# Mask products first, then score and value products by alternating halves of the array, in a kernel for one step of a hybrid decoder

## The chip, the cores and the metric

The kernel runs on one core of a Trainium2 chip. The metric is the device time of one execution in microseconds (us). In the profile PE is TensorE's matmuls, PEld its weight loads, DVE VectorE, ACT ScalarE, POOL GpSimd, SP the engine that issues most DMAs.

## The reference

One layer of a decoder with two head groups works on 272 prompt positions (16 learned meta tokens and 256 of the prompt) and 8 sample sequences of one new token each. Cut to what matters here:

```python
z = h @ w_in                                  # u | q | k | v
y_ssm = s5_mixer(u, ...)                      # state-space heads
# sliding-window attention, 16 query heads of 64 on 4 key/value heads
s = einsum('bnqkgd,bnskd->bnkgqs', qb, k2) * HEAD_DIM ** -0.5
s = where(mask, s, -1e30)                     # causal, window 128
p = softmax over the keys and one learned sink per head
o = einsum('bnkgqs,bnskd->bnqkgd', p, v2)
x = x + concat(rmsnorm(y_ssm), rmsnorm(o)) @ w_out
x = x + conv_ffn(rmsnorm(x))                  # 2048 -> 2 x 5632 -> 2048
```

The meta positions, the prompt and the sample tokens go through the same layer; the attention of the sample tokens runs over a cache of 128 keys.

## The kernel before

Activations stand with features on the partitions and the 280 positions as columns. Every projection (`project`) takes its weights in chunks of 512 KB: one DMA to `w`, a rounding copy `wh` on ScalarE (L216) and the remainder `wl` on VectorE (L72 by way of `sub`), and then three products for each block, wh with the high part of the input, wh with the low part, wl with the high part (`mm3`, L233 to L235, tile `acc`). One chunk is 24 such matmuls in the attention stage. There are two buffers each of wh, wl and acc.

The attention of the prompt is done in eight groups (`att_group`), one for each of four key/value heads kv and of two blocks of 128 queries. Kind A, the first block, has 144 keys (16 meta keys with the values vM, which lie in the tile vx, and 128 with the values vA); kind B, the second, has 256 keys (vA and vB). A group has four query heads r and runs in four steps, with a `yield` between them:

1. Scores in the PSUM tile `sps`, two banks of 2 x 256 columns; head r goes to bank r % 2. For each head a bf16 product of the identity and the mask `maskb` writes the mask (L840), with all 128 rows of the array, and an fp32 product of `qT` and `kd` adds the scores (L841). Head dimension 64 fills half of the rows: heads 0 and 2 the lower half, heads 1 and 3 the upper.
2. Softmax: maximum on VectorE (L849), exponential on ScalarE (L856), sums, reciprocal (L860), scaling on ScalarE (L862). P has one buffer.
3. Eight transposes to `ppt` (L870) and two copies to `pt` on ScalarE (L873). sps and ppt share two PSUM buffers ("big").
4. Values in the one PSUM tile `ops` (L879): for each half `par` of the output partitions, that is of the array's columns, the two blocks of keys are accumulated. `att_out` then reads it with ScalarE and VectorE (L810, L811, L814).

All fp32 products run as two passes; a row of the trace that has x2 for one product in the code shows them.

TensorE's order is the order of the code (`manual_schedule`); the other engines' orders are set by the scheduler's priorities. The main loop (L1004) writes step 1 of a group, projection chunks of u (`us`, counted by the table UD), steps of the sample's and the meta tokens' attention (`side`, tiles ssp, p, osp and mps, mtp, mop), step 3 of the group before, step 2 of this one, again chunks of u, and step 4 of the group before. Between them VectorE builds tables for the state-space part (BB, CC) in pieces of low priority.

The stage lies between the projections of q and the state-space part. Behind it come the state-space part mixed with the output projection of the attention (oa), the gate, the rest of the output projection and the feed-forward part, which take 220 to 1200 us.

Of the kernel before, what the change touches and what calls it, by code (L numbers as in the profile page):

```python
# [65 lines left out]
def body(ctx, tc, I, O, dbg=None):  # L66
    nc = tc.nc
    dbg = dbg or {}
    V, A, G, PE = nc.vector, nc.scalar, nc.gpsimd, nc.tensor

    def tt(o, a, b, op, eng=V):
        return eng.tensor_tensor(o, a, b, op=op)  # L72

    def add(o, a, b, eng=V):
        return tt(o, a, b, OP.add, eng)
# [4 lines left out]
    def mul(o, a, b, eng=V):  # L80
        return tt(o, a, b, OP.mult, eng)
# [51 lines left out]
    identb = ap.tile([128, 128], BF, name="identb")  # L133
    G.tensor_copy(identb, ident)
    mf = stp.tile([128, 256], F32, name="mf")
    maskb = {}
# [167 lines left out]
    qT = buf[:, 0:8, :]  # L304
    bflat = buf.rearrange("p f n -> p (f n)")
    b8_ = bflat[:, 8 * NR:]
    kd = b8_[:, :4 * T].rearrange("p (f n) -> p f n", f=4)
# [497 lines left out]
    def att_out(f, src, c, n):  # L805

        m = src.shape[1]
        for a in range(m):
            g = vcol("attn_out_g", f + a)
            A.activation(ah[:, f + a, c:c + n], src[:, a], AF.Copy, scale=g)  # L810
            V.scalar_tensor_tensor(al[:, f + a, c:c + n], src[:, a], g, ah[:, f + a, c:c + n].bitcast(F32),  # L811
                                   op0=OP.mult, op1=OP.subtract)
        z = small.tile([128, T], F32, name="osqt", tag="tb")[:, :m * n].rearrange("p (a b) -> p a b", a=m)
        A.activation(z, src, AF.Square)  # L814
        o = osq[:, c:c + n]
        if f == 0:
            add(o, z[:, 0], z[:, 1], eng=G)
        for a in range(2 if f == 0 else 0, m):
            add(o, o, z[:, a], eng=G)
# [11 lines left out]
    def att_group(nm, kv):  # L831
        ci = 0 if nm == "A" else 1
        q0 = QC[ci][1]
        nk = 144 if nm == "A" else 256
        k0 = 0 if nm == "A" else 16
        sps = big.tile([128, 2, 2, 256], F32, name="sps", tag="big")
        for r in range(4):
            h = 4 * kv + r
            p = slice(64 * (h % 2), 64 * (h % 2) + 64)
            PE.matmul(sps[:, r % 2, r // 2, :nk], identb, maskb[nm][:, :nk], start=True, stop=False)  # L840
            PE.matmul(sps[:, r % 2, r // 2, :nk], qT[p, h // 2, q0:q0 + 128], kd[p, kv, k0:k0 + nk], start=False, stop=True)  # L841
        st = aw.tile([128, 8, 4], F32, name="st")
        mx, nm_, se, den, rec = (st[:, i, :] for i in range(5))
        yield
        hp = tc.high_priority()
        hp.__enter__()
        sk = sinks[:, 4 * kv:4 * kv + 4]
        sc = rq[:, 16 * ci + 4 * kv:16 * ci + 4 * kv + 4]
        V.tensor_reduce(mx.rearrange("p (a b) -> p a b", b=2), sps[:, :, :, :nk].rearrange("p b a k -> p a b k"),  # L849
                        axis=AX.X, op=OP.max)  # L850
        mul(nm_, mx, nrq[:, 16 * ci + 4 * kv:16 * ci + 4 * kv + 4])
        tt(nm_, nm_, nsk[:, 4 * kv:4 * kv + 4], OP.min)
        add(se, sk, nm_)
        P = aw.tile([128, 4, 256], F32, name="P", bufs=1)
        for r in range(4):
            A.activation(P[:, r, :nk], sps[:, r % 2, r // 2, :nk], AF.Exp, scale=sc[:, r:r + 1], bias=nm_[:, r:r + 1],  # L856
                         accum_out=den[:, r:r + 1])
        A.activation(se, se, AF.Exp)
        add(den, den, se)
        V.reciprocal(rec, den)  # L860
        for r in range(4):
            A.activation(P[:, r, :nk], P[:, r, :nk], AF.Copy, scale=rec[:, r:r + 1])  # L862
        hp.__exit__(None, None, None)
        yield
        blocks = ((0, 16, vM), (16, 128, vA)) if nm == "A" else ((0, 128, vA), (128, 128, vB))
        pts = []
        ppt = big.tile([128, 2, 4, 128], F32, name="ppt", tag="big")
        for bi, (c, n, vv) in enumerate(blocks):
            for r in range(4):
                PE.transpose(ppt[:n, bi, r, :], P[:, r, c:c + n], ident)  # L870
        for bi, (c, n, vv) in enumerate(blocks):
            pt = aw.tile([128, 4, 128], F32, name="pt")
            A.copy(pt[:n], ppt[:n, bi])  # L873
            pts.append(pt)
        yield
        ops = msc.tile([128, 2, 128], F32, name="ops", tag="msc")
        for par in range(2):
            for bi, (c, n, vv) in enumerate(blocks):
                PE.matmul(ops[64 * par:64 * par + 64], vv[:n, 64 * kv:64 * kv + 64], pts[bi][:n, par::2, :],  # L879
                          start=bi == 0, stop=bi == 1)  # L880
        att_out(2 * kv, ops, q0, 128)
        yield
# [65 lines left out]
    def att_meta():  # L948
# [41 lines left out]
        yield  # L990

    gs_ = [att_group(nm, kv) for nm in ("A", "B") for kv in range(4)]
    sg, mg = att_sample(), att_meta()
    def side(k):
# [437 lines left out]
```

## Time and profile before

| | |
|---|---|
| median of 3 runs | 1202.74 us (1202.39 to 1205.45) |
| profiled execution | 1202.62 us, span of its instructions 1200.4 us |
| PE busy | 1172.8 us, 98% of the span |
| PEld, DVE, ACT, POOL busy | 94%, 68%, 51%, 8% |
| granted TensorE clock, mean | 0.987 of 2.4 GHz |
| DMA | 201.90 MB, 168 GB/s |

In a timeline a row is one instruction or a run of like ones: its start, its length, what it writes and reads, how many there are, and in brackets how long the engine sat idle before it and which instruction ended that. Matmuls overlap each other, so what one costs is read from the start of a row to the start of the next and not from its length.

### The profile page before, as it was taken

The numbers are of one execution on the slowest core, as the hardware profiler recorded it, in microseconds if no ns is written. First come the engines' busy times: TensorE is split into PE (matmuls) and PEld (weight loads), VectorE is DVE, ScalarE is ACT, GpSimd is POOL, SyncE is SP. The second block draws the span as 40 slices with busy tenths as digits, with TensorE's granted clock in tenths as the row PEclk, the third lists the DMA queues.
The fourth block names the chain that finished last, engine by engine and source line by source line (L and its number), as shares of the span: only waits on it lengthen the run. The fifth ranks groups of instructions, "written<-read, shape, count | busy, mean of one in ns | idle before, by whom it ended". The sixth has DMA issues, their size and how long they took to land.

```text
span 1200.4 us, 23033 instructions
## 1 busy us (share of the span) xinstructions
PE 1172.8 (98%) x9184; PEld 1133.7 (94%) x9184; DVE 813.0 (68%) x1469; ACT 608.4 (51%) x1009; POOL 97.1 (8%) x243
## 2 busy tenths in 40 slices
PE   7999999899998999999999999999999999999998
PEld 6887878799997999999999999999999999999998
DVE  8798767488778967676767644446767676764443
ACT  5567557566564654454445433334445444543332
POOL 1020121322014200000000000000000000000000
PEclk9999889799999999999999999999999999999999
DMA  8445344434465655555555555555555555556664
GB/s 272 142 140 169 98 129 145 135 87 118 114 184 158 193 160 178 179 179 180 178 176 176 169 181 187 180 182 178 180 181 179 178 176 176 176 187 199 201 198 128
DMA packets 237114, 201.90 MB, mean 168 GB/s; under 512 B 16152, under 2 KB 233256, under 8 KB 236968
## 3 DMA queue, kind: packets, MB, share of 16 engines
q1 hardware_dynamic: 233856, 193.88, 52.9%
q10 hardware_dynamic: 2608, 3.58, 0.9%
q0 software_dynamic: 544, 2.97, 0.7%
q8 instruction: 72, 1.18, 0.5%
q14 instruction: 34, 0.28, 0.1%
HBM read 194.59 MB, written 8.25 MB: 169 GB/s over the span
## 4 chain that ended last, share of the span: by engine, by line
PE 91%; DVE 3%; ACT 3%; issue 1%; DMA 1%; SPq 0%; POOL 0%; ACTq 0%; DVEq 0%; POOLq 0%
PE acc L233 27%; PE acc L235 26%; PE acc L234 26%; PE yps L1136 2%; PE sps L841 2%; PE kvb L571 1%; DVE wl L72 1%; PE ops L879 1%; PE kps L1077 1%; ACT wh L216 1%; PE ppt L870 1%; PE vps L1095 1%; PE sps L840 1%; PE lps L1067 0%; DMA w<-w_in 0%
## 5 line engine op out<-in xcount | busy, mean ns | idle before, releaser
L72 DVE TENSOR_TENSOR wl<-w,wh 128x1024 fp32r<-128x1024 f32 (+1 forms) x348 | 419.8, 1206 | 306.4 <-ACT wh L216 302.2
L216 ACT CAST wh<-w 128x1024 fp32r<-128x1024 f32 (+1 forms) x348 | 358.2, 1029 | 493.4 <-PE acc L234 332.4
L233 PE MATMUL acc<-x2h,wh 128*128 128x266 f32 x1408 | 397.0, 287 | 0.7 <-DVE os L72 0.7
L234 PE MATMUL acc<-x2l,wh 128*128 128x266 f32 x1408 | 395.7, 286 | 0.0
L235 PE MATMUL acc<-x2h,wl 128*128 128x266 f32 x1408 | 375.0, 287 | 0.0
L234 PEld LDWEIGHTS acc<-x2l,wh 128*128 128x128 f32 x1408 | 267.1, 190 | 0.1
L233 PEld LDWEIGHTS acc<-x2h,wh 128*128 128x128 f32 x1408 | 265.9, 189 | 0.9 <-issue 0.9
L235 PEld LDWEIGHTS acc<-x2h,wl 128*128 128x128 f32 x1408 | 254.2, 189 | 0.1
L234 PE MATMUL acc<-hl,wh 128*128 128x264 f32 x704 | 196.1, 284 | 0.0
L233 PE MATMUL acc<-hh,wh 128*128 128x264 f32 x704 | 196.0, 284 | 0.0
L235 PE MATMUL acc<-hh,wl 128*128 128x264 f32 x704 | 184.2, 284 | 0.0
L234 PEld LDWEIGHTS acc<-hl,wh 128*128 128x128 f32 x704 | 132.3, 188 | 0.0
L233 PEld LDWEIGHTS acc<-hh,wh 128*128 128x128 f32 x704 | 132.3, 188 | 0.0
L235 PEld LDWEIGHTS acc<-hh,wl 128*128 128x128 f32 x704 | 126.1, 188 | 0.0
L233 PE MATMUL acc<-xh,wh 128*128 128x266 f32 (+1 forms) x256 | 78.8, 308 | 0.0
L235 PE MATMUL acc<-xh,wl 128*128 128x266 f32 (+1 forms) x256 | 75.9, 296 | 1.7 <-DVE wl L72 1.5
L234 PE MATMUL acc<-xl,wh 128*128 128x266 f32 (+1 forms) x256 | 75.8, 296 | 0.0
L1314 POOL COPY coll<-up 128x10 f32<-128x10 f32 x88 | 16.9, 192 | 634.1 <-DVE up L72 633.9
L233 PEld LDWEIGHTS acc<-xh,wh 128*128 128x128 f32 x256 | 50.3, 196 | 4.4 <-issue 3.4
L235 PEld LDWEIGHTS acc<-xh,wl 128*128 128x128 f32 x256 | 49.9, 195 | 2.4 <-DVE wl L72 2.3
L234 PEld LDWEIGHTS acc<-xl,wh 128*128 128x128 f32 x256 | 50.2, 196 | 0.1
L1317 ACT ACTIVATE ct<-up,cin 128x256 f32<-128x256 f32 x88 | 48.1, 594 | 0.0
(371 smaller groups left out, 1579.5 us busy)
## 6 DMA issues: line engine op xcount, KB each, us to landing
w<-w_up SPq DMA_DIRECT2D x176, 512.0 KB, 3.5
w<-w_down SPq DMA_DIRECT2D x64, 512.0 KB, 3.4
w<-w_in SPq DMA_DIRECT2D x40, 512.0 KB, 3.7
w<-w_out SPq DMA_DIRECT2D x32, 512.0 KB, 3.8
w<-w_down SPq DMA_DIRECT2D x32, 384.0 KB, 3.2
w<-w_glu SPq DMA_DIRECT2D x8, 512.0 KB, 3.7
buf<-x_t SPq DMA_DIRECT2D x4, 532.0 KB, 6.8
out_y<-buf ACTq DMA_DIRECT2D x8, 264.0 KB, 4.1
```

The costliest lines, as they stand in the source:

```text
L72: return eng.tensor_tensor(o, a, b, op=op)
L216: A.copy(wh[:, :nk, :], w[:, :nk, :])
L233: PE.matmul(ps, wh, xh, start=st, stop=False)
L234: PE.matmul(ps, wh, xl, start=False, stop=False)
L235: PE.matmul(ps, wl, xh, start=False, stop=sp)
L571: PE.matmul(kv_ps[f], kw[b][:, j, cc], xs[:, b + j, :], start=b + j == 0, stop=False)
L840: PE.matmul(sps[:, r % 2, r // 2, :nk], identb, maskb[nm][:, :nk], start=True, stop=False)
L841: PE.matmul(sps[:, r % 2, r // 2, :nk], qT[p, h // 2, q0:q0 + 128], kd[p, kv, k0:k0 + nk], start=False, stop=True)
L870: PE.transpose(ppt[:n, bi, r, :], P[:, r, c:c + n], ident)
L1136: PE.matmul(yps[:, r, :], lhs, rhs, start=part == 0, stop=part == 2)
L1314: G.tensor_copy(coll[:, n, :], up[:, NR - 10:NR])
L1317: A.activation(t, up[:, 2:258], AF.Identity, scale=cin[:, n, 2:3], bias=cin[:, n, 3:4])
```

## The change

All mask products of a group come first: one for each bank, with the mask read twice by a broadcast, so two products of 2 x nk columns instead of four of nk. The four score products follow, one behind the other, and only the last one on each bank closes its accumulation. In the values' products the two loops change places: block by block, the two halves of the columns one after the other.

```diff
         sps = big.tile([128, 2, 2, 256], F32, name="sps", tag="big")
+        for b in range(2):
+            PE.matmul(sps[:, b, :, :nk], identb, maskb[nm][:, None, :nk].to_broadcast([128, 2, nk]), start=True, stop=False)
         for r in range(4):
             h = 4 * kv + r
             p = slice(64 * (h % 2), 64 * (h % 2) + 64)
-            PE.matmul(sps[:, r % 2, r // 2, :nk], identb, maskb[nm][:, :nk], start=True, stop=False)
-            PE.matmul(sps[:, r % 2, r // 2, :nk], qT[p, h // 2, q0:q0 + 128], kd[p, kv, k0:k0 + nk], start=False, stop=True)
+            PE.matmul(sps[:, r % 2, r // 2, :nk], qT[p, h // 2, q0:q0 + 128], kd[p, kv, k0:k0 + nk], start=False, stop=r >= 2)
...
         ops = msc.tile([128, 2, 128], F32, name="ops", tag="msc")
-        for par in range(2):
-            for bi, (c, n, vv) in enumerate(blocks):
+        for bi, (c, n, vv) in enumerate(blocks):
+            for par in range(2):
                 PE.matmul(ops[64 * par:64 * par + 64], vv[:n, 64 * kv:64 * kv + 64], pts[bi][:n, par::2, :],
                           start=bi == 0, stop=bi == 1)
```

Lines behind the change are numbered one higher in the changed kernel (L841 becomes L842, L879 becomes L880).

On TensorE, the scores of the first group of kind A before, from the last small products ahead of them (qtp), for two of the four heads:

```order
L772 MATMUL qtp<-ones,qd 128x1
L840 LDWEIGHTS identb
L840 MATMUL sps<-maskA,identb 128x144
L841 MATMUL sps<-buf 128x144
L840 LDWEIGHTS identb
L840 MATMUL sps<-maskA,identb 128x144
L841 MATMUL sps<-buf 128x144
```

The same place now, with the whole group and the projection behind it (buf is the tile that holds qT and kd):

```order
L772 MATMUL qtp<-ones,qd 128x1
L838 LDWEIGHTS identb
L838 MATMUL sps<-maskA,identb 128x2x144
L838 LDWEIGHTS identb
L838 MATMUL sps<-maskA,identb 128x2x144
L842 MATMUL sps<-buf 128x144 x4
L233 MATMUL acc_1265<-xh,wh 128x280
```

Masks and scores no longer alternate, and the four score products stand in a row.

On TensorE, the values of the first group of kind A before, between a projection and the next group's mask:

```order
L235 MATMUL acc_1422<-xh,wl 128x280
L879 MATMUL ops<-pt,vx 64x256
L879 MATMUL ops<-pt,vA 64x256
L879 MATMUL ops<-pt,vx 64x256
L879 MATMUL ops<-pt,vA 64x256
L840 LDWEIGHTS identb
```

And now:

```order
L235 MATMUL acc_1418<-xh,wl 128x280
L880 MATMUL ops<-pt,vx 64x256 x2
L880 MATMUL ops<-pt,vA 64x256 x2
L838 LDWEIGHTS identb
L838 MATMUL sps<-maskA,identb 128x2x144
```

Products of the same block are now neighbours; in kind B the same holds for vA and vB.

On ScalarE, whose order the scheduler sets, before, from the table load ahead of the first exponentials to the second group's scaling:

```order
L856 ACT_TABLE_LOAD
L856 ACTIVATE P,st<-sps,st,rq 128x144 x4
L858 ACTIVATE st<-st 128x4
L216 CAST wh<-w 128x1024
L862 ACTIVATE P<-P,st 128x144 x4
L858 ACTIVATE st<-st 128x4
L856 ACTIVATE P,st<-sps,st,rq 128x144 x4
L873 COPY pt<-ppt 16x512
L873 COPY pt<-ppt 128x512
L216 CAST wh<-w 128x1024
L967 ACTIVATE mS<-mS 2x256
L969 ACTIVATE mst<-mst 2x16
```

And now:

```order
L857 ACT_TABLE_LOAD
L857 ACTIVATE P,st<-sps,st,rq 128x144 x4
L859 ACTIVATE st<-st 128x4
L216 CAST wh<-w 128x1024
L863 ACTIVATE P<-P,st 128x144 x2
L859 ACTIVATE st<-st 128x4
L863 ACTIVATE P<-P,st 128x144 x2
L857 ACTIVATE P,st<-sps,st,rq 128x144 x4
L874 COPY pt<-ppt 16x512
L874 COPY pt<-ppt 128x512
L968 ACTIVATE mS<-mS 2x256
L970 ACTIVATE mst<-mst 2x16
```

The head of the row is the same; the weight cast that stood behind the copies of pt has moved behind the next group's scaling.

## Rows read from the trace of the kernel before

**Rows 1.** The page, the chain that ended last: shares of the span by engine.
```profile
PE 91%; DVE 3%; ACT 3%; issue 1%; DMA 1%; SPq 0%; POOL 0%; ACTq 0%; DVEq 0%; POOLq 0%
```

**Rows 2.** Waits of PE, 104.7 to 217 us: total, times, longest.
```profile
PE ppt L870 <- ACT P L862: 0.9, 1, 0.9
```

**Rows 3.** Busy time by stretch: PE, PEld, DVE, ACT, POOL; granted clock; DMA.
```profile
104.70:141.05 36.35, 35.39 (x267) 28.04 (x267) 30.62 (x93) 27.48 (x67) 4.09 (x7) 1.00 0.46 137
141.05:147.90 6.85, 6.85 (x27) 5.77 (x27) 3.28 (x9) 0.39 (x1) 1.04 (x2) 0.51 0.25 73
161.50:164.90 3.40, 3.40 (x17) 3.40 (x16) 2.45 (x7) 2.89 (x10) 1.93 (x4) 0.50 0.48 152
175.20:182.00 6.80, 6.80 (x24) 4.97 (x24) 3.65 (x9) 1.07 (x2) 2.16 (x4) 0.50 0.62 183
178.35:194.98 16.63, 16.63 (x101) 14.09 (x102) 14.17 (x32) 8.58 (x23) 2.81 (x6) 0.89 0.37 107
104.70:217.00 112.30, 110.66 (x717) 86.67 (x716) 81.43 (x213) 69.93 (x183) 20.03 (x40) 0.90 0.47 145
```

**Rows 4.** Timeline of PE: scores of the first group of kind A.
```profile
104.78 0.24 PE L840 MATMUL sps<-maskA,identb 128*128 128x144 bf16 x1
104.95 0.51 PE L841 MATMUL sps<-buf 64*128 64x144 f32 x2
105.39 0.24 PE L840 MATMUL sps<-maskA,identb 128*128 128x144 bf16 x1
...
107.21 0.40 PE L233 MATMUL acc<-xh,wh 128*128 128x280 f32 x1
```

**Rows 5.** Timeline of PE: scores of a group of kind B.
```profile
188.29 0.28 PE L235 MATMUL acc<-xh,wl 128*128 128x280 f32 x1
188.42 0.28 PE L840 MATMUL sps<-maskB,identb 128*128 128x256 bf16 x1
188.63 0.70 PE L841 MATMUL sps<-buf 64*128 64x256 f32 x2
189.26 0.28 PE L840 MATMUL sps<-maskB,identb 128*128 128x256 bf16 x1
...
191.78 0.40 PE L233 MATMUL acc<-xh,wh 128*128 128x280 f32 x1
```

**Rows 6.** PE, 116.11 to 116.14; statistics of L952 (ns, min/median/max); the first transposes.
```profile
116.12 0.18 PE L952 MATMUL mps<-buf 64*2 64x16 f32 x2
...
L952 PE MATMUL mps<-buf x32: 172/173/175, 116.1 to 116.5; 64*2 64x16 f32 x32
...
117.56 1.63 PE L870 MATMUL ppt<-ident,P 128*16 128x128 f32 x8 [0.88 <-ACT P L862]
```

**Rows 7.** Timeline of PE: values of the first group of kind A.
```profile
122.21 0.64 PE L879 MATMUL ops<-pt,vx 16*64 16x256 f32 x2
122.78 0.65 PE L879 MATMUL ops<-pt,vA 128*64 128x256 f32 x2
...
124.50 0.24 PE L840 MATMUL sps<-maskA,identb 128*128 128x144 bf16 x1
```

**Rows 8.** Timeline of PE: values of the first group of kind B.
```profile
184.21 0.66 PE L879 MATMUL ops<-pt,vA 128*64 128x256 f32 x4
184.69 0.61 PE L879 MATMUL ops<-pt,vB 128*64 128x256 f32 x4
185.23 0.40 PE L233 MATMUL acc<-xh,wh 128*128 128x280 f32 x1
```

**Rows 9.** Timeline of ACT before the first transposes.
```profile
111.88 1.28 ACT L856 ACT_TABLE_LOAD   x1
...
116.14 1.04 ACT L216 CAST wh<-w 128x1024 fp32r<-128x1024 f32 x1 [0.95 <-ACT st L858]
117.09 1.33 ACT L862 ACTIVATE P<-P,st 128x144 f32<-128x144 f32 x4
```

**Rows 10.** Timeline of DVE: scaling of the sample's probabilities.
```profile
194.23 0.28 DVE L925 TENSOR_SCALAR Ps<-Ps,sst 128x128 f32<-128x128 f32 x1
```

## The prediction

> **What bounds the kernel now.** I read the page first, for the share of each engine and the chain that ended last: 91% of it is TensorE [rows 1]. Nearly all of that is the projections, which the change leaves alone; the touched work lies in the attention stage, 104.7 to 217 us, so I then read that stretch by stages and by waits. There the longest wait of TensorE is 0.9 us [rows 2]; VectorE is busy 81.4 and ScalarE 69.9 of the 112.3 us [rows 3]. What TensorE saves there is therefore saved for the whole program, until another engine is late. After the stage the order of every engine is the same in both programs, and the feed-forward part that follows is TensorE's, so what is left at 217 us I carry to the end unchanged. Three stretches of the stage, 6.85, 3.40 and 6.80 us long, ran at half the clock (granted 0.50 to 0.51: 1.2 instead of 2.4 GHz) with TensorE busy throughout [rows 3]. Last I read the touched instructions one by one.
>
> **Scores.** In a group of kind A (144 keys) one head takes 0.17 us from the start of its mask product to that of its scores, and 0.44 from there to the next mask; four take 104.78 to 107.21, 2.43 us [rows 4]. In kind B (256 keys) the two are 0.21 and 0.63, and the group 3.36 [rows 5]. The difference of 112 columns gives the price of a column: 0.04/112 = 0.36 ns in the mask product, and 0.19/224 = 0.85 ns in one pass of the scores (each score product is two passes, the x2 of its row). What is left is fixed: 0.12 us for a mask product and 0.195 for a score product (0.44 - 288 x 0.85 ns). In the projections, where one full-array product follows another, a row starts 0.13 us after the last [rows 5], so the fixed part is hidden there; here it is paid at each change between the full array and a half of it, eight times in a group.
>
> After the change a group has one such change and back. Kind A: two mask products of 288 columns, 0.12 + 2 x 0.104 = 0.33 us (0.12 more if the second one's load isn't hidden). Then four score products, two on each half of the rows. Do the halves run side by side? The 32 meta products alternate halves in the same way: two that start at 116.12 together end 0.18 us later [rows 6], one alone takes 0.173 [rows 6], so they start at most 10 ns apart, less than the 16 x 0.85 = 14 ns in which one streams its columns. I take yes. Then the four cost 0.195 + 4 x 144 x 0.85 ns = 0.685, and the group 1.01 instead of 2.43: **1.42 saved**. In turn they would cost 1.175, with 0.93 saved. Kind B: 0.12 + 2 x 0.184 + 0.195 + 4 x 256 x 0.85 ns = 1.55 instead of 3.36: **1.81 saved**, 0.94 in turn. Four groups of each: 4 x (1.42 + 1.81) = **12.9 us**, lower end 7.5.
>
> **Values.** In kind A the four products start 0.57 us apart, 122.21 to 124.50, 2.29 in all [rows 7]: two passes of 256 columns at 0.85 ns are 0.435, the other 0.135 fixed, since vx fills 16 rows and vA 128 and each product follows one of the other kind. The change puts the two halves of vx together and then the two of vA. Two halves of one kind run side by side already: in kind B, whose two blocks both have 128 rows, the old order vA, vB, vA, vB shows as four passes of vA from 184.21 and four of vB from 184.69, done by 185.23, 1.02 us in all [rows 8], where eight passes in turn would be 1.74. So kind A becomes two pairs of 0.57, 1.14: 1.15 saved, four times, **4.5 us** after 0.02 for each pair's offset (ends 0, if halves of 16 rows don't pair, and 5.1, if it becomes as fast as B). In kind B I expect nothing.
>
> All this takes it that a pass may start ahead of earlier ones of the other half, as the four-and-four of [rows 8] shows: the program's order there is two passes of vA and two of vB on one half and then the same on the other. The Trainium skill (TensorE: Matmul & The Clock Gate, Part 3, What overlaps and what doesn't) says that matmuls start and end strictly in program order; the trace speaks against it here, and what it would make of the time is the fifth rival.
>
> **What is given back.** Sum so far 17.4 us of TensorE. Three items where another engine is then late:
> - The first transposes, ppt at 117.56, waited 0.88 us for the scaled probabilities [rows 6]. ScalarE's table load begins at 111.88; then come the exponentials and one weight cast, which stood 0.95 us until a projection freed its buffer; then the scaling, 117.09 to 118.4 [rows 9]. TensorE comes 2 x 1.42 = 2.84 us earlier, ScalarE only by that 0.95 (the scheduler still has table load, exponentials, cast and scaling in this order, and puts the next cast behind the second scaling). **1.9 lost.** The next values hang on that transpose by the exponentials and the copies of the probabilities, so they don't regain it.
> - The transpose of the sample's probabilities, p, needs VectorE's product Ps, started at 194.23 [rows 10], behind the products that build CC. From 178.35 to 194.98 VectorE works 14.2 of 16.6 us [rows 3]. TensorE would need 16.6 - 1.8 (scores) - 1.8 (half of the 3.65 us at half clock up to 182.0) = 13.0. At 14.5 for VectorE **1.5 lost** (0 if the clock stays, 2.6 if its idle time stays too).
> - The rest of the stage: TensorE goes from 112.3 to about 90 us, VectorE keeps its 81. I allow **1.5** (0 to 4) for scalings, copies and weight parts that come late.
>
> **The clock.** Each of the three falls came where no projection had run for some time: values, the 16 meta transposes and scores up to 141.05; scores, 16 sample products and transposes up to 161.5; values, sample products and scores up to 175.2. Projections brought it back. They cost half of 6.85 + 3.40 + 6.80, 8.5 us [rows 3]. The first of these stretches shrinks to about half (2.29 and 2.43 us of it become 1.14 and 1.01), so I take its 3.4 as won; of the others (5.1), whose sample products stay, half; and 1 is lost to a new fall at the longer wait before the first transposes: **+5.0** (ends 0 and 8.5).
>
> Sum: 12.9 + 4.5 - 1.9 - 1.5 - 1.5 + 5.0 = 17.5. The profiled execution took 1202.62 us (2.2 outside its span), and the median of the runs is 1202.74, so no correction is needed: 1202.6 - 17.5 = **1185.1 us**.
>
> **Rivals.**
> 1. The row halves of the scores take turns. For it: the meta products have two columns of weights, the scores 128, so loads may collide. Against: the pairs of [rows 6, 8]. Scores give 7.5 instead of 12.9, and the shorter stretch leaves 0.8 less to wait for: 12.9 us, 1189.7.
> 2. The clock falls as often as before, since the sample products that precede two falls stay. Then no 5.0, but also no wait at p: 14.0 us, 1188.6.
> 3. VectorE or ScalarE bounds the stage. In 104.7 to 141.05 VectorE is busy 30.6 of 36.35 us [rows 3] and TensorE would fall to 29 or 30. If its order of small and large products makes TensorE wait in each of the eight groups by the 1 us of [rows 9], 8 us go instead of 1.5 + 1.5: 12.5 less what a slower stretch also costs in clock, about 2: 10.5, 1192.1.
> 4. Slower than before: each wait that TensorE now runs into lets the clock fall, and the next chunk of projections (24 rows at 0.13, 3.1 us) runs at half of it, 3.1 us each. The other savings without clock gain are 12.5, so it decides from five such falls on, over those of before, and passes the measurable 0.3% at six: 12.5 - 6 x 3.1 = -6.1, 1208.7. Against it: at today's wait of 0.9 us [rows 2] the granted clock of its stretch is 1.00 [rows 3].
> 5. Passes start in program order only. The two passes of one product lie on one half, so the other half starts a pass late: five passes instead of four in a group of scores, three instead of two in a pair of values of kind A. 4 x (0.12 + 0.22) + 8 x 0.22 = 3.1 less: 14.4, 1188.2. It is what the page named above says; [rows 8] speaks against it.
> The change not doing what it says would be the first rival together with no gain in the values: 17.5 - 4.6 - 4.5 = 8.4, 1194.2.
>
> **How the numbers follow.** Forecast 0.65; rival 1 0.09, 2 0.13, 3 0.07, 4 0.02, 5 0.02, not doing what it says 0.02. A measurement of this kernel tells about 0.3% (3.6 us) from no change. The forecast's own bounds: best, values 5.1, clock 8.5, waits 2.4 in all, 12.9 + 5.1 + 8.5 - 2.4 = 24; worst, clock 1 and waits 7, 12.9 + 4.5 + 1 - 7 = 11.4. For 8 in 10 I cut the best end to 23, since all three ends seldom meet, and let the slow end reach rivals 1 to 3: 1179.5 to 1193.0. Faster by over 0.3%: all but rival 4 and the far tail of 3, 0.95; within it 0.03; slower 0.02.
>
> **What would show it.** Right: score groups near 1.0 and 1.55 us from first mask to the next instruction; the four score products as two pairs that start within some 10 ns; values of kind A near 1.2, of kind B still 1.02; a wait of 2 to 3 us before the first transposes; fewer or shorter stretches at half clock; everything after the stage shifted as a whole. Wrong: score groups of 1.5 and 2.4 (rival 1); three stretches at half clock of the old length (2); waits of TensorE on VectorE's and ScalarE's weight parts or probabilities of over 8 us in the stage (3).

## The result and the profile after

The changed kernel takes **1184.22 us** (median of 4 runs, 1183.48 to 1186.19) where the kernel before took 1202.61 beside it: 0.9844 of it, with a 95% interval of 0.9825 to 0.9863. The prediction was 1185.1 us. The profiled execution took 1183.48 us, with a span of 1181.5.

TensorE still bounds the kernel, by a smaller share of the chain [rows 1]:

```profile
PE 88%; DVE 6%; ACT 3%; issue 1%; DMA 1%; SPq 0%; POOL 0%; ACTq 0%; DVEq 0%; POOLq 0%
```

The timeline of PE, the first groups of kind A and of kind B [rows 4, 5]:

```profile
103.74 0.42 PE L838 MATMUL sps<-maskA,identb 128*128 128x288 bf16 x2
104.09 0.76 PE L842 MATMUL sps<-buf 64*128 64x144 f32 x8
104.78 0.40 PE L233 MATMUL acc<-xh,wh 128*128 128x280 f32 x1
...
145.53 0.60 PE L838 MATMUL sps<-maskB,identb 128*128 128x512 bf16 x2
146.07 1.13 PE L842 MATMUL sps<-buf 64*128 64x256 f32 x8
147.13 0.50 PE L901 MATMUL ssp<-Qb,KT 128*128 128x8 f32 x3
```

From the first mask product to the next instruction, a group of kind A takes 1.04 us instead of 2.43, one of kind B 1.60 instead of 3.36. A look at 20 ns of the same line shows why four products of 144 columns need so little. Two passes start within them; in `s_onehalf` below, where all four products lie on one half, it is a single pass:

```profile
104.09 0.39 PE L842 MATMUL sps<-buf 64*128 64x144 f32 x2
```

Values of kind A and of kind B [rows 7, 8]:

```profile
121.24 0.65 PE L880 MATMUL ops<-pt,vx 16*64 16x256 f32 x4
121.82 0.65 PE L880 MATMUL ops<-pt,vA 128*64 128x256 f32 x4
122.40 0.42 PE L838 MATMUL sps<-maskA,identb 128*128 128x288 bf16 x2
...
166.49 0.65 PE L880 MATMUL ops<-pt,vA 128*64 128x256 f32 x4
166.97 0.60 PE L880 MATMUL ops<-pt,vB 128*64 128x256 f32 x4
167.50 0.40 PE L233 MATMUL acc<-xh,wh 128*128 128x280 f32 x1
```

Kind A went from 2.29 to 1.16 us. Kind B stayed: 1.02 before, 1.01 now, and its rows read alike ([rows 8]) although the program's order of its four products changed.

Waits of TensorE in the stage (a view of 100 to 226 us: total, times, longest) [rows 2]:

```profile
PE ppt L871 <- ACT P L863: 1.9, 1, 1.9
PE ops L880 <- ACT osqt L814: 1.0, 1, 1.0
...
PE acc L235 <- DVE wl L72: 0.5, 1, 0.5
...
PE p L929 <- DVE st L72: 0.4, 1, 0.4
```

The wait at the first transposes has grown from 0.9; the values' wait for osqt (the last reader of the one buffer of ops), the one for a weight part wl and the one at p are new. Behind the stage the wait at orps, the norm of the attention's output, went from 3.3 to 4.0 us.

Busy time by stretch (PE, PEld, DVE, ACT, POOL; granted clock; DMA) [rows 3]:

```profile
104.00:183.00 79.00, 76.19 (x611) 64.10 (x610) 73.67 (x194) 59.27 (x154) 17.03 (x25) 0.96 0.50 149
115.28:118.69 3.41, 3.20 (x13) 2.47 (x14) 3.41 (x11) 2.02 (x9) 0.00 (x0) 0.50 0.64 180
159.65:163.07 3.42, 3.42 (x15) 2.60 (x16) 3.42 (x7) 0.75 (x2) 0.00 (x0) 0.50 0.89 263
190.37:200.61 10.24, 9.56 (x44) 8.03 (x44) 2.99 (x9) 4.35 (x14) 7.29 (x19) 0.50 0.93 305
204.03:210.85 6.82, 4.78 (x22) 4.72 (x23) 2.34 (x12) 2.52 (x5) 0.83 (x2) 0.50 0.01 2
```

Of the three stretches at half clock of before, 17.05 us, two are gone and one of 3.42 us is left; one of 3.41 is new, from the first transposes on. In the tail of the stage there are two, 10.24 and 6.82 us. Before, these two were (same columns, kernel before):

```profile
212.73:219.56 6.83, 6.16 (x26) 4.48 (x24) 2.39 (x7) 4.12 (x12) 6.29 (x17) 0.50 0.77 251
222.97:229.80 6.83, 6.23 (x27) 6.12 (x28) 2.35 (x12) 1.51 (x4) 0.82 (x2) 0.50 0.16 29
```

The first row of after holds the point that decided the experiments: VectorE is busy 73.7 of these 79 us, TensorE 76.2. The same work, from the first score group to the seventh transposes, before and now:

```profile
104.78:203.54 98.76, 97.80 (x628) 76.17 (x627) 74.75 (x195) 60.84 (x156) 13.38 (x25) 0.91 0.40 119
...
103.74:182.91 79.17, 76.36 (x612) 64.11 (x611) 73.83 (x194) 59.44 (x154) 17.03 (x25) 0.96 0.50 149
```

VectorE's work stayed at 74 us while the stretch shrank from 98.8 to 79.2.

### The profile page after: what moved, and what is told of

It is laid out like the page before. It is cut to its first block, busy times and chain, and to the rows that moved or that the text cites. A ratio compares the mean times of both kernels' runs of the same rounds, so it can differ in the third digit from the quotient of the medians.

```text
span 1181.5 us, 23002 instructions
## 1 busy us (share of the span) xinstructions
PE 1151.0 (97%) x9168; PEld 1122.0 (95%) x9168; DVE 812.1 (69%) x1469; ACT 607.9 (51%) x1009; POOL 102.2 (9%) x243
## 4 chain that ended last, share of the span: by engine, by line
PE 88%; DVE 6%; ACT 3%; issue 1%; DMA 1%; SPq 0%; POOL 0%; ACTq 0%; DVEq 0%; POOLq 0%
PE acc L235 26%; PE acc L233 26%; PE acc L234 26%; PE yps L1137 2%; DVE wl L72 2%; PE kvb L571 1%; PE kps L1078 1%; DVE w L72 1%; PE vps L1096 1%; ACT wh L216 1%; PE lps L1068 1%; PE ppt L871 1%; PE ops L880 1%; PE osp L939 0%; DMA yd<-ysb 0%
```

## The experiments

Each is a change to the changed kernel. `again` below is that kernel itself, run once more as a measure.

### 1. Each part alone: s_only and v_only

```diff
 # s_only
-        for bi, (c, n, vv) in enumerate(blocks):
-            for par in range(2):
+        for par in range(2):
+            for bi, (c, n, vv) in enumerate(blocks):
 # v_only
-        for b in range(2):
-            PE.matmul(sps[:, b, :, :nk], identb, maskb[nm][:, None, :nk].to_broadcast([128, 2, nk]), start=True, stop=False)
...
-            PE.matmul(sps[:, r % 2, r // 2, :nk], qT[p, h // 2, q0:q0 + 128], kd[p, kv, k0:k0 + nk], start=False, stop=r >= 2)
+            PE.matmul(sps[:, r % 2, r // 2, :nk], identb, maskb[nm][:, :nk], start=True, stop=False)
+            PE.matmul(sps[:, r % 2, r // 2, :nk], qT[p, h // 2, q0:q0 + 128], kd[p, kv, k0:k0 + nk], start=False, stop=True)
```

> The changed scores alone (mask products first, four score products in a row), the values' products in their old order. My theory is that a group's gain is the product of two things, fewer changes between the full array and a half of it, and halves that run side by side. By it a score group takes 1.04 us in kind A and 1.60 in kind B, as in the changed kernel, which saves 4 x (1.39 + 1.76) = 12.6 us, and a pair of values in kind A is back at 2.29. Of the clock: if the falls are set by the length of a stretch of small products, the stretch of values, meta transposes and scores near 130 to 140 us is longer again by 1.15 us and may fall once more (3.4 us lost); if the scores' share was enough, it stays at full clock. 1188 to 1192 us, about 1189 without the fall. A rival, that the gain comes mainly from the clock and not from the products, would give score groups over 2 us or a time above 1194.

Measured: 1189.82 us, 0.9888 (0.9871 to 0.9904). Score groups 1.04 and 1.60 us, pairs of values 2.29. The stretch near 130 to 140 us stays at full clock.

> The changed order of the values' products alone, the scores as before. My theory: two pairs of like halves, 1.16 us instead of 2.29 in each of the four groups of kind A, nothing in kind B (1.02 us as before), so 4.5 us; no earlier arrival at the first transposes, so no new wait and no half-clock stretch there. With the old falls 1198; if the shorter stretch up to 141 us keeps the full clock, 3.4 less, 1194.7. If what the two parts bring adds up, the gains of this kernel and of the one with the scores alone sum to the 18.4 us of the whole change; if the clock wants both parts, the sum is smaller by one or two stretches of 3.4 us. A rival, that halves with 16 rows of weights and 128 rows do not pair, would leave the group of kind A at over 1.7 us and the time within 2 us of before.

Measured: 1194.28 us, 0.9933 (0.9914 to 0.9953). Values of kind A in 1.16 us; the half-clock stretch at 141 us is 3.41 us long instead of 6.85:

```profile
140.29:143.70 3.41, 3.41 (x17) 3.41 (x16) 3.08 (x9) 0.38 (x1) 1.03 (x2) 0.50 0.28 86
```

Both products' gains are real by themselves. The two gains, 12.7 and 8.2 us against the same runs of before, sum to 20.9 where the whole change gives 18.4. The intervals are some 2 us each way, so the surplus of 2.5 is not settled; its sign would fit if what TensorE saves beyond a point is met by waits (experiment 3), which is not shown for these two. What falls is the idea that the clock wants both parts together: that would have made the sum smaller than the whole.

### 2. What makes a score group short: s_order and s_onehalf

```diff
 # s_order
-        for r in range(4):
+        for r in (0, 2, 1, 3):
 # s_onehalf
-            p = slice(64 * (h % 2), 64 * (h % 2) + 64)
+            p = slice(0, 64)
```

> The changed kernel with the four score products of a group in the order 0, 2, 1, 3: first both on the lower half of the rows, then both on the upper half. My theory, that passes of one half may run ahead of earlier ones of the other half, gives the same groups, 1.04 and 1.60 us, with starts in pairs; the time within 1 us of the changed kernel, 1183.5 to 1185. If passes start in program order only, the first upper pass waits for three lower ones: seven pass times in place of four (the two halves overlap in one), so 0.37 us more in kind A (1.41) and 0.65 more in kind B (2.25): 4.1 us more, about 1188.

The timeline of PE of this kernel, kind A and kind B:

```profile
104.48 0.42 PE L838 MATMUL sps<-maskA,identb 128*128 128x288 bf16 x2
104.83 0.77 PE L842 MATMUL sps<-buf 64*128 64x144 f32 x8
105.52 0.40 PE L233 MATMUL acc<-xh,wh 128*128 128x280 f32 x1
...
146.59 0.60 PE L838 MATMUL sps<-maskB,identb 128*128 128x512 bf16 x2
147.12 1.14 PE L842 MATMUL sps<-buf 64*128 64x256 f32 x8
148.19 0.28 PE L901 MATMUL ssp<-Qb,KT 128*128 128x8 f32 x1
```

1.04 and 1.60 us again, and 1184.5 us in all (one run): with both heads of the lower half ahead of both of the upper, the groups take no longer. Passes of the second half start ahead of four earlier ones of the first. The Trainium skill (TensorE: Matmul & The Clock Gate, Part 3, What overlaps and what doesn't) says that matmuls keep the program's order in start and end. The measurement decides: here it does not hold. The expectation put a group of kind A whose passes start in program order at 1.41 us, so the fifth rival falls.

> The changed kernel, but all four heads read the lower half of the rows, so that heads 1 and 3 compute scores from the data of heads 0 and 2; everything else is as in the changed kernel. It takes away the pairing and keeps the mask products in front. My theory: eight passes in turn at 0.85 ns a column, 4 x 0.12 us more in kind A and 4 x 0.22 more in kind B beyond the paired ones, so about 1.53 and 2.47 us a group, and 4 x (0.49 + 0.87) = 5.4 us more in all, less what the wait before the first transposes takes back (1 us), 1188 to 1189. If the groups stay at 1.04 and 1.60, the halves never ran side by side and the gain was the changes of mode alone. If they reach 2.4 and 3.3, the pairing was all of it.

```profile
104.04 0.42 PE L838 MATMUL sps<-maskA,identb 128*128 128x288 bf16 x2
104.39 1.25 PE L842 MATMUL sps<-buf 64*128 64x144 f32 x8
105.56 0.40 PE L233 MATMUL acc<-xh,wh 128*128 128x280 f32 x1
...
145.75 0.61 PE L838 MATMUL sps<-maskB,identb 128*128 128x512 bf16 x2
146.29 1.99 PE L842 MATMUL sps<-buf 64*128 64x256 f32 x8
148.21 0.28 PE L901 MATMUL ssp<-Qb,KT 128*128 128x8 f32 x1
```

1.52 and 2.46 us: the gain of the scores comes apart into two measured halves. Masks in front, without pairing, bring 2.43 - 1.52 = 0.91 in kind A and 3.36 - 2.46 = 0.90 in kind B, 7.2 us in eight groups. That it is the same in both kinds shows it as fixed cost, 0.3 us for each of the three changes to the full array and back that are gone. What in such a change costs is not taken apart: each is also one between a bf16 and an fp32 product, and two of the four mask products are gone with them. That a change of rows costs something by itself is seen in kind A's old order of the values, where all products are fp32: 0.57 us from vx (16 rows) to vA (128 rows) [rows 7], against 0.48 from vA to vB, both of 128 rows [rows 8]. The Trainium skill (TensorEngine Tiling (Array Packing), Key Properties) says that changing the tiling mode drains TensorE and gives no price; the 0.3 us for a round trip agree with it, though no run shows that a drain is what they are.

Pairing brings the rest, 0.48 and 0.86, 5.4 us. The kernel took 1187.37 us (one run), 3.2 more than the changed one and not 5.4. Part of that is seen: TensorE waits 1.3 instead of 1.9 us at the first transposes, hardly for wl and not at p, and no stretch at half clock follows the transposes. Against it, stretches of 3.41 us from 150.25 and of 20.48 from 194.62 bring the half clock to 27.3 us, where the changed kernel has 23.9. The items don't add up to the 3.2, and the rest stays open.

### 3. The new waits: ud_first, ud_last, out_hp

```diff
 # ud_first
-    UD = ((1, 1, 0), (2, 1, 0), (1, 1, 0), (0, 2, 0), (0, 1, 1), (1, 1, 0), (0, 1, 0), (0, 0, 0))
+    UD = ((2, 1, 0), (1, 1, 0), (1, 1, 0), (0, 2, 0), (0, 1, 1), (1, 1, 0), (0, 1, 0), (0, 0, 0))
 # ud_last
+    UD = ((1, 1, 0), (2, 1, 0), (1, 1, 0), (0, 2, 0), (0, 1, 1), (1, 0, 0), (0, 1, 0), (1, 0, 0))
 # out_hp
-        att_out(2 * kv, ops, q0, 128)
+        with tc.high_priority():
+            att_out(2 * kv, ops, q0, 128)
```

> The changed kernel with one more chunk of u projections ahead of the first transposes and one less in the second round (table UD, first two entries exchanged); the number of chunks is the same. My theory: TensorE waits 1.9 us there because ScalarE comes with the scaled probabilities only at 115.5 us, and the wait makes the clock fall for 3.4 us behind it. With 3.1 us of work put into that place the wait is gone and so is the half-clock stretch (1.7 us): up to 3.6 us less than the changed kernel, 1180.6 to 1182.5, if no wait grows at the second transposes, which lose that cover. A rival: ScalarE and VectorE have the weight parts of the extra chunk to make first, so the probabilities come later by as much, the wait stays over 1.2 us and the time within 1 us of the changed kernel.

Measured: 1184.95 us, 0.986 (0.9844 to 0.9877), no gain. The first transposes wait for nothing and the clock stays up (113 to 121 us: granted 1.00), and at the sixth values TensorE is 3.9 us ahead (176.40 instead of 180.29). At the transposes behind them, the seventh, it stands:

```profile
182.93 2.53 PE L871 MATMUL ppt<-ident,P 128*128 128x128 f32 x8 [3.85 <-ACT P L863]
```

182.93 is where these transposes stood in the changed kernel too (182.91). ScalarE and VectorE ahead of it, in this kernel:

```profile
178.42 1.05 ACT L216 CAST wh<-w 128x1024 fp32r<-128x1024 f32 x1
182.37 1.71 ACT L863 ACTIVATE P<-P,st 128x256 f32<-128x256 f32 x4 [0.91 <-DVE st L861]
...
179.50 1.23 DVE L72 TENSOR_TENSOR wl<-w,wh 128x1024 fp32r<-128x1024 f32 x1 [1.55 <-ACT wh L216]
180.98 1.21 DVE L850 TENSOR_REDUCE st<-sps 128x4 f32<-128x1024 f32 x1
182.11 0.17 DVE L861 RECIPROCAL st<-st 128x4 f32<-128x4 f32 x1
```

The reciprocal that the scaling needs stands behind a weight part and the next group's maximum, and VectorE was idle for 1.55 us ahead of that weight part, until ScalarE had made its cast: here the order of the two engines counts, beside the sum of their work. Neither the theory nor the rival as written down was right: the wait went from the first place, and came back larger at another.

> The changed kernel with one chunk of u projections moved from the sixth round to the last, so that it stands ahead of the last values and the 32 sample products behind them (osp, 5.73 us at half clock in the changed kernel, 3.59 before). My theory: small products without projections between them for long let the clock fall; a chunk among them keeps it up, so the osp block is back at 3.6 us or less and the stretch of 10.2 us is 3.4 us shorter at least: 1.7 to 3 us less, 1181 to 1182.5. A rival: the stretch only moves, since the sixth round now has less projection between its values and its scores; then a half-clock stretch of the same length appears near 175 to 185 us, and the time stays within 1 us of the changed kernel, or the wait at the sample's transpose p grows to over 2 us and it is slower by 1 to 2 us.

Measured: 1183.88 us, 0.9852 (0.9837 to 0.9867). The rival's first case was right in the place and in the time, though not in the length: osp takes 1.81 + 1.70 us and the clock stays up from 189 to 199, but TensorE now waits 2.9 us for the sixth group's pt, and a stretch of 3.41 us at half clock follows there (180.75 to 184.16).

```profile
180.62 1.03 PE L880 MATMUL ops<-pt,vA 128*64 128x256 f32 x4 [2.91 <-ACT pt L874]
```

> The changed kernel with the reading of a group's values (ScalarE and VectorE, lines 811 to 815) at the scheduler's high priority, so that the one PSUM buffer of ops is free sooner. My theory: the wait of 1.0 us of the values at 188.1 us for osqt is a matter of ScalarE's order alone, since the scheduler now puts that read behind the next group's exponentials; with it in front the wait goes and 1 us is saved, 1183 to 1183.5. A rival: the exponentials then come later by the 1 us that they gave way, and the next transposes wait instead; no difference of over 0.5 us. Which of the two, is read from the waits of TensorE; the time alone will hardly tell.

Measured: 1182.65 us, 0.9835 (0.9821 to 0.985). The values at 187.73 us wait no longer for osqt, and no other wait of TensorE in the stage grew, so the theory fits; the intervals of this kernel and of the changed one overlap, so a gain of 1 us is not shown by the time.

### 4. Is it VectorE? again, g_cc, uf_g, uf_g_hp, uf_halfcc

```diff
 # g_cc
-            mul(w2, Nb, pi)
+            mul(w2, Nb, pi, eng=G)
...
-            mul(w2, Rb, pi)
+            mul(w2, Rb, pi, eng=G)
 # uf_halfcc
+    G.memset(CC[:, 16:], 0.0)
...
-        for h in range(0, 32, 8):
+        for h in range(0, 16, 8):
```

uf_g is g_cc with the table UD of ud_first, uf_g_hp is uf_g with the edit of out_hp, and uf_halfcc has the table of ud_first too.

> The changed kernel itself, once more, as the measure for the three versions beside it on the same chip. 0.9844 of before as the first time, 1183 to 1185 us; in its profile score groups of 1.04 and 1.60 us, a wait of 1.9 us before the first transposes and 20 to 28 us at half clock in all.

Measured: 1184.34 us, 0.9846 (0.9831 to 0.986). Where its trace differs in the stage from the first one: there is no stretch at half clock near 160 us. That brought nothing, since TensorE then stood 1.9 us at p:

```profile
PE p L929 <- DVE st L72: 1.9, 1, 1.9
...
140.00:177.10 37.10, 35.23 (x279) 29.74 (x279) 36.35 (x86) 26.68 (x70) 9.29 (x17) 1.00 0.51 147
```

From the first score group to p it is 72.4 us with the stretch at half clock (176.09 - 103.74) and 72.6 without (177.10 - 104.54). VectorE is busy 36.4 of the 37.1 us up to p: with its work in this order, VectorE sets when p comes.

> The changed kernel with 8 of the 24 products that build the table CC (w2, 128 x 512) on GpSimd instead of VectorE. VectorE is busy 73.7 of the 79 us from 104 to 183 in the changed kernel, TensorE waits little there. My theory: VectorE is the next engine to be late, but in the changed kernel only at one or two places (the transpose of p, 0.7 us, the weight part wl, 0.5 us), so 5.5 us less work on it gains 0.5 to 1.2 us and no more: 1183 to 1184. A rival: VectorE already sets the pace of the whole stretch, and relief of it gives 3 us or more. Another: GpSimd takes over 2 us for each, the chain of each CC piece gets longer and the time rises.

Measured: 1186.71 us, 0.987 (0.985 to 0.9889), 2.4 us more than `again` beside it. That is the direction of the third expectation, though GpSimd takes 1.4 us for a product and not over 2; the two intervals just overlap (0.985 to 0.986), so that it is slower is likely and not settled. VectorE's own products of CC, grouped by shape, in `again`, and then in g_cc with two rows of the timelines of GpSimd and VectorE:

```profile
L72 DVE TENSOR_TENSOR w<-CC,PW 128x512 f32<-128x512 f32 x16 | 10.3, 684 | 0.0
```

```profile
L72 DVE TENSOR_TENSOR w<-CC,PW 128x512 f32<-128x512 f32 x8 | 8.0, 1004 | 0.1
...
162.98 1.06 POOL L72 TENSOR_TENSOR w<-CC,PW 128x512 f32<-128x512 f32 x1 [0.76 <-DVE CC L72]
...
163.08 1.51 DVE L72 TENSOR_TENSOR w<-CC,PW 128x512 f32<-128x512 f32 x1
```

A product of 0.68 us took 1.51 when it started 0.1 us after one of GpSimd, and ended 0.55 us after that one did. Half of the 16 products were gone from VectorE (the 24 of the expectation count the 8 sums too), and the rest took half as long again, so these products relieved it by 2.3 us instead of 5.5. Where the time went is seen on TensorE: it waits 3.35 us for a weight part at 175.31, the one that took VectorE 2.08 us from 173.18, and 6.83 us from 173.16 on are at half clock.

> Both: one more chunk of projections before the first transposes, and a third of the CC products on GpSimd. With the extra chunk alone, TensorE ran 3.2 us ahead up to 172 us and then stood 3.8 us at the seventh transposes (182.9 us) since the probabilities came no earlier than without it: small products of the softmax stood behind large ones on VectorE, which was busy 75.2 of 79 us. My theory: with VectorE relieved by 5.5 us the probabilities come earlier, the wait at the seventh transposes falls under 1.5 us and the gain of the extra chunk is kept: 1181 to 1182.5. A rival: the order on VectorE and ScalarE is what is late, not the sum of their work (exponentials, cast, then the sums behind a weight part); then the wait stays at 3 us or more and the time at 1184 to 1185.

Measured: 1184.57 us, 0.9848 (0.9833 to 0.9864). The seventh transposes wait no more, but the values just before them stand 3.5 us for pt. The time is the rival's, the place of the wait neither's. Since VectorE was hardly relieved, this didn't tell the theory from the rival.

> All three edits in one: the extra chunk ahead of the first transposes, a third of the CC products on GpSimd, and the reading of the values at high priority. If the three gains add up (3.2 at the start, 1 at the seventh values, 1 from VectorE) it takes 1179 to 1181 us. If each only moves the wait to another place, it is within 1 us of the changed kernel: then the stage is at the bound of VectorE and ScalarE and not of TensorE's order.

Measured: 1182.31 us, 0.9827 (0.9812 to 0.9843): the lowest of the kernels that compute all, but its interval overlaps that of the changed kernel. It lies between the two expectations: the three gains don't add up to 1179 to 1181, and at 2.0 us below `again` it isn't within 1 us either.

> The version with the extra chunk of projections ahead of the first transposes, and half of the table CC left out: its second half is set to zero by GpSimd beforehand instead of being computed, so 8 products and 4 sums of 128 x 512 (about 8 us) are gone from VectorE and the state-space outputs of half the channels are not the reference's. It takes VectorE's load away without giving it to GpSimd, whose products made VectorE's own CC products take 1.0 to 1.2 us instead of 0.68. Theory: VectorE's sum of work is what is late at 176 to 183 us, so the wait of 3.8 us at the seventh transposes falls under 1.5 us, p is not waited for, and the time is 1180 to 1182. A rival: the order on ScalarE and VectorE (cast and weight part ahead of the sums of the softmax) makes the wait; then it is still 3 us or more at that place and the time 1184 to 1185.

Measured: 1178.83 us, 0.9802 (0.9786 to 0.9819), against 0.986 for ud_first. With 8 us of products and sums gone from VectorE some 6 us are gone from the whole, and of the kernels here this alone is faster than the changed one with no overlap of the intervals. The same 79 us in ud_first and in uf_halfcc:

```profile
104.00:183.00 79.00, 74.62 (x613) 63.32 (x612) 75.16 (x200) 59.48 (x154) 14.62 (x25) 0.98 0.51 152
```

```profile
104.00:183.00 79.00, 76.31 (x637) 64.84 (x636) 68.55 (x185) 61.88 (x160) 12.07 (x26) 1.00 0.52 154
...
177.79 0.18 DVE L862 RECIPROCAL st<-st 128x4 f32<-128x4 f32 x1
...
178.09 0.65 PE L881 MATMUL ops<-pt,vA 128*64 128x256 f32 x4 [1.62 <-ACT pt L875]
```

The wait of 3.85 us is gone, the largest left in that stretch is 1.62, and the clock is 1.00 throughout. So taking work off VectorE was enough to end the wait that swallowed the gain of ud_first. Whether the sum of the work did it or the order isn't separated, because the edit changed both. In ud_first the seventh group's exponentials end at 178.54 and the reciprocal starts at 182.11, behind weight part and maximum; here they end at 177.56, and the reciprocal (L862 in this kernel) follows at 177.79 with neither in between. Of the 6 us, two stretches at half clock that this kernel doesn't have, 6.8 us in all, would make up to 3.4, an estimate at half of their length.

## Why the prediction was right, point by point

| term | predicted | measured in the profiles |
|---|---|---|
| scores | 12.9 | 4 x (2.43 - 1.04) + 4 x (3.36 - 1.60) = 12.6 |
| values of kind A, of kind B | 4.5, 0 | 4 x (2.29 - 1.16) = 4.5, 0 |
| wait at the first transposes | -1.9 | -1.0, and -0.5 for wl just before |
| wait at p | -1.5 | -0.6 (idle before p 0.13 to 0.73) |
| rest of the stage | -1.5 | -1.0 (osqt) |
| clock, three stretches of the stage | +5.0 | (17.05 - 3.42 - 3.41)/2 = +5.1 |
| clock in the tail | 0 | (13.66 - 17.06)/2 = -1.7 |
| sum | 17.5 | 17.4 |

The two profiles lie 19.1 us apart, the medians 18.4. Of the difference to 17.4, 1.0 is the start: the first group began at 103.74 in this profile and at 104.78 in that of before, and it began anywhere from 103.67 to 104.91 in the others, whatever the kernel; that isn't the change. The other 0.7 is open. Half of a stretch at half clock is the most that it can cost, since TensorE also waits in it: in the two of the tail it was busy 12.4 us before and 14.3 now, which makes -1.0 instead of -1.7, and the wait at orps took another 0.7.

That the two sums agree to 0.1 is luck. The waits came 1.8 us smaller than put down, and the tail, put down at nothing, took 1.7 back.

**Scores and values** were read right: the price of a column and the fixed price of a change from the rows of two kinds, and pairing from other products that already had it. Experiment 2 shows both halves of that argument by themselves, and that the first and the fifth rival are not what happens. The half without pairing came to 7.2 where 7.5 stood as the lower end. The fixed price was put down to the change between the full array and a half; by experiment 2 that is its place, but not yet its cause.

**The first transposes** waited for the cause that was named, in the order that was named (the timeline of ACT, [rows 9]):

```profile
110.84 1.28 ACT L857 ACT_TABLE_LOAD   x1
...
114.04 1.04 ACT L216 CAST wh<-w 128x1024 fp32r<-128x1024 f32 x1
115.01 0.72 ACT L863 ACTIVATE P<-P,st 128x144 f32<-128x144 f32 x2
```

The cast no longer waits. TensorE came to the products just ahead, mps, 2.0 us earlier by the distance from the first scores (9.33 instead of 11.34 us) and not the 2.84 put down, since the projection chunk ahead of them, with a wait for wl in it, took 4.05 instead of 3.28 us. So the wait is 1.9, where 2 to 3 us were named. The fall of the clock there, put down at 1 us, cost 1.7.

**p** waited less than predicted in the profile after, because a stretch at half clock ahead of it (159.65 to 163.07) took the time; in `again` the clock stayed up and the wait was there. The prediction said that these two exclude each other, and these two profiles show it. One bound of this item doesn't follow from its row: with VectorE's 2.5 idle us kept, the loss would be 16.6 - 13.0 = 3.6 and not 2.6; nothing else in the sum hangs on it.

**The clock** term is right in size, but two of its own guesses cancel: of the two later stretches 3.4 us were won where 2.55 stood, and 1.7 instead of 1 was lost at the new one. The tail was the step that failed: the prediction gave it no change of the clock, and there the 32 osp products ran mostly at half clock (5.73 us instead of 3.59). They stand behind the wait for osqt, but `out_hp` has a stretch of the same 10.24 us (190.96 to 201.20) without that wait, so its cause stays open. `ud_last` has 17.1 us at half clock up to 226 us instead of 23.9 and takes the same time, with 2.9 us of wait at the sixth values: fewer stretches there brought nothing either.

**The third rival** (VectorE bounds the stage) is not what decides this change, at 0.9844, but it comes near to the truth for the next one: what ud_first had gained was lost at probabilities for which TensorE waits on ScalarE and VectorE, and only less work on VectorE brought time beyond the intervals.

## What to carry to other kernels

Products that use half of the array belong next to each other, one half beside the other, and apart from those that use all of it; the fixed price of a change is read by comparing two shapes of the same product, and whether halves pair by looking for products that already alternate. When the bounding engine is to be relieved in a stage, look up the busy share of the second engine in that stage first: here VectorE went from 75 of 99 us to 74 of 79, and from then on moving chunks of TensorE's work only moved the waits. Before giving VectorE's work to GpSimd, see whether the two run side by side at all.

## What the runs showed of the chip that was not expected

- Two products of 128 x 512 on VectorE and GpSimd that read SBUF did not run side by side: in `g_cc` 0.68 us became 1.51, and a weight part wl of 1.21 us 2.08. The Trainium skill (SBUF — State Buffer, Who interferes with whom) says that an instruction of VectorE with two SBUF inputs contends with one of GpSimd that reads SBUF, and calls the shared pair of ports an exclusive lock. That the row of 1.51 us ends 0.55 us behind GpSimd's, near the 0.68 that it takes alone, agrees with it.
- Passes of one half of the array overtook four earlier ones of the other half, loads and products alike, with no loss (`s_order`: 1.04 us in either order).
- A wait of about 1.8 us before the first transposes was followed by a stretch at half clock in six of seven profiles that had it, and waits of 0.9 and 1.3 us in none of the three that had those. Which stretches fall differs between two profiles of one kernel, at the same time in all (1184.2 and 1184.3 us), and a stretch of 3.4 us far behind the stage, between 353 and 373 us, stands in the profiles of eleven of the fourteen runs, `again` among them, and not in those of before, of the changed kernel's first and of `s_onehalf`. So a single stretch of a single profile is weak evidence of a cause.
